# Five pairs of gate columns by a seven-product scheme in a two-block transformer kernel, with other buffer counts

## The chip, the cores and the metric

The kernel runs on one core of a Trainium2 chip, as one program in one launch. The metric is the device time of one execution in microseconds. Engines are named as in the profile: PE (TensorE), DVE (VectorE), ACT (ScalarE), POOL (GpSimd), SP (SyncE, which issues the weight loads).

## The reference, cut to what matters

Two transformer blocks over 512 tokens of width 1024 in fp32. The first block (a gated mixer with a delta rule, cross attention over a memory, a squared-ReLU feed-forward) is not touched by the change other than through buffer counts. The second block is:

```python
u = rmsnorm_2(x, norm_mix_w[l])
proj = u @ w_in[l] + b_in[l]
cb, cc, cx, q, k, v, g_conv, g_attn = jnp.split(proj, IN_SPLITS, axis=-1)
y_conv = (cb * causal_dwconv_2(cc * cx, conv_mix_w[l])) @ w_conv_out[l]
...
y_attn = sliding_window_attention(q, k, v, sinks[l]) @ w_attn_out[l] + b_attn_out[l]
merged = jax.nn.sigmoid(g_conv) * y_conv + jax.nn.sigmoid(g_attn) * y_attn
x = x + merged @ w_mix_out[l]
u = rmsnorm_2(x, norm_ffn_w[l])
up, gate = jnp.split(u @ w_ffn_up[l], 2, axis=-1)
a = causal_dwconv_2(up, ffn_conv_w[l], ffn_conv_b[l])
x = x + (jax.nn.silu(a) * gate) @ w_ffn_down[l]
```

The gates `g_conv` and `g_attn` are 1024 wide each: in columns of 128 they are columns 30 to 37 and 38 to 45 of `w_in_2`.

## The kernel before, in words

Activations are held transposed: a tile is 128 features by 512 tokens, and x is eight such tiles. Every matrix product runs in three matmuls per block of 128 x 128 weights (`mm3`, L480 to L484): weights and activations are split into a high part (rounded to fp32r) and a low part (the rest), and high x high, high x low and low x high are summed in PSUM. ACT makes the high part, DVE subtracts it to get the low part.

Weights come in units of eight blocks (128 x 1024), in one order written by `weight_order` (L60). SP loads them into NRAW = 4 raw buffers; `prefetch` (L256) splits them into one of NWS = 5 pairs of tiles `whi` and `wlo`. A plain column of `w_in_2` is one unit: eight blocks, 24 matmuls of 512 columns.

Two neighbouring columns can be a *pair*: `weight_order` lists it with `pair`, which orders the 16 blocks as quarters, and `pairg` (L367) computes it as a 2 x 2 block product with seven block products instead of eight (84 matmuls of 256 columns). For that, `seven_steps` (L309) forms two combinations of the weights (`sraw`, NSR = 2 buffers) and splits three tiles of 1024 and one of 512; `rights` (L413) forms the combinations of the activations, once for all pairs that share them, in steps s0 (two scalings by ACT), s1 (five short instructions of DVE) and s2 (two splits), for each two of the eight tiles. The seven products land in four PSUM banks (kind "mm" or "sm", four banks each), and L407 to L410 recombine them into a tile `q` of 1024 columns (NQ = 2 buffers), which a function `then` reads. Before the change pairs stand in the first block's feed-forward (14) and in the second one's (12, `SEVEN2`).

All tiles of 128 x 512 share one pool of NSLOT = 67 slots (`t2`, `tmp`, `acc_tile`). A slot is given when a tile is first written and comes free after its last reader.

What sets the order: the text issues instructions in its own order, `defer(n, f)` puts work n blocks of weights later, and the Tile framework then gives each engine a fixed order at build time, in which an instruction can run ahead of the text where its inputs are ready and it needs no new tile. SP alone keeps the order of the text. At run time each engine works through its queue in order.

In the second block's mixer, generators feed PE while the attention's chain waits (L1663 to L1667): `kvq_g`, `conv2_g` (columns 0 to 23), and `gated_g` (L1640): column 30, the eight columns of `w_conv_out_2`, then columns 31 to 37, each followed by a drain with rb (L1457), a sigmoid (L1659) and a product with `yc` (L1660). `norm_x` (L1441), eight instructions that apply the first block's last norm to x in place, is written beside them. Then (L1670 to L1677) each of columns 38 to 45 is followed by four blocks of `w_attn_out_2`, two DVE instructions with the gate (L1675, L1676) and a split of `yc` (L1677). The columns of `w_mix_out_2` follow (L1680), which add to x.

Of the kernel before, what the change touches and what calls it, by code (L numbers as in the profile page):

```python
# [13 lines left out]
AF = mybir.ActivationFunctionType  # L14
# [4 lines left out]
T = 512  # L19
D = 1024  # L20

NSLOT = 67
NRAW, NWS = 4, 5

NSR, NQ = 2, 2


SPREAD = [6, 2]
# [31 lines left out]
def weight_order():  # L60


    seq = []
    seven = set()

    def pair(name, n1, n2):
        assert len(seq) % 8 == 0
        seven.add(len(seq) // 8)
        for n, o in ((n1, 0), (n2, 1), (n1, 1), (n2, 0)):
            for k in range(o, 8, 2):  # L70
                seq.append((name, k, n))

    def cols(name, ns, ks):
        for n in ns:
            for k in ks:
                seq.append((name, k, n))

    def rows(name, ks, ns):
        for k in ks:
            for n in ns:  # L80
                seq.append((name, k, n))

    r8 = range(8)
    for lo in (12, 8, 16):
        cols("w_in", range(lo, lo + 4), r8)
    rows("w_in", r8, range(4, 8))
    cols("w_in", range(0, 4), r8)
    cols("w_in", range(20, 24), r8)
    cols("xa_wk", r8, r8)
    rows("xa_wv", r8, range(4))  # L90
    rows("xa_wv", r8, range(4, 8))
    cols("w_out", range(NWO), range(4))
    cols("w_out", range(NWO), range(4, 8))
    cols("w_out", range(NWO, 8), r8)
    cols("xa_wq", r8, r8)
    cols("xa_wo", range(4), range(6))
    cols("xa_wo", range(4), (6, 7))
    cols("xa_wo", range(4, 8), r8)
    for what, i, g in ffn_order():
        if what == 1 and i < NPLAIN:  # L100
            cols("ffn_w1", (2 * i, 2 * i + 1), r8)
        elif what == 1:
            pair("ffn_w1", 2 * i, 2 * i + 1)
        else:
            cols("ffn_w2", [i], range(8 * g, 8 * g + 8))

    cols("w_in_2", [28, 29, 24, 25, 26, 27], r8)
    for i in range(8):
        cols("w_in_2", [8 + i, 16 + i, i], r8)
    cols("w_in_2", [30], r8)  # L110
    cols("w_conv_out_2", r8, r8)
    cols("w_in_2", range(31, 38), r8)
    for i in range(8):
        cols("w_in_2", [38 + i], r8)
        cols("w_attn_out_2", [i], range(4))
    cols("w_mix_out_2", r8, r8)
    for what, i, g in ffn2_order():
        if what == 2:
            cols("w_ffn_down_2", [i], range(*GROUPS2[g]))
        elif i in SEVEN2:  # L120
            pair("w_ffn_up_2", i, 22 + i)
        else:
            cols("w_ffn_up_2", [i, 22 + i], r8)
    cols("w_ffn_down_2", r8, range(*GROUPS2[2]))
    return seq, seven
# [64 lines left out]
def _build(ctx, tc, nc, A, out, stage):  # L190
# [5 lines left out]
    V, S, G, PE = nc.vector, nc.scalar, nc.gpsimd, nc.tensor  # L196
    cnt = [0]

    def nm(s):
        cnt[0] += 1  # L200
        return f"{s}_{cnt[0]}"

    def t2(dt=F32, shape=(P, T)):
        return ap_.tile(list(shape), dt, tag="t2", bufs=NSLOT, name=nm("t2"))

    def ch(dt=F32):
        return ap_.tile([P, 4, P], dt, tag="t2", bufs=NSLOT, name=nm("ch"))

    def tmp(shape=(P, T)):
        return ap_.tile(list(shape), F32, tag="t2", bufs=NSLOT, name=nm("tmp"))  # L210

# [3 lines left out]
    def tinyc(n):  # L215
        return ap_.tile([P, n], F32, tag=nm("tinyc"), bufs=1, name=nm("tinyc"))
# [16 lines left out]
    def load_x():  # L233
        r = []
        for k in range(8):
            xt = ap_.tile([P, T], F32, tag="t2", bufs=NSLOT, name=nm("res"))
            nc.sync.dma_start(out=xt, in_=A["xT"][k])
# [3 lines left out]
    def col(name, i=0, n=1):  # L241
        o = COFF[name][0] + i
        return colt[:, o:o + n]
# [166 lines left out]
        V.tensor_tensor(q4[:, 1:3, :], b3(3), q4[:, 1:3, :], op=ALU.add)  # L410
        then(q)

    def rights(x, gname, xs):  # L413


        H = T // 2
        f = lambda hl, j: (hl[0][:, j * H:(j + 1) * H], hl[1][:, j * H:(j + 1) * H])
        res = [{} for _ in range(len(xs) // 2)]
        steps = []

        def one(p):
            st = {}

            def s0():
                st["a"], st["b"] = t2(), t2()
                S.activation(st["a"], x[2 * p], AF.Copy, scale=col(gname, 2 * p))
                S.activation(st["b"], x[2 * p + 1], AF.Copy, scale=col(gname, 2 * p + 1))

            def s1():
                a, b = st["a"], st["b"]  # L430
                st["v"], st["w"] = v, w = t2(), t2()
                V.tensor_sub(v[:, H:], b[:, H:], a[:, H:])
                V.scalar_tensor_tensor(out=w[:, :H], in0=a[:, H:], scalar=1.0, in1=a[:, :H],
                                       op0=ALU.mult, op1=ALU.subtract)
                V.tensor_scalar_mul(v[:, :H], w[:, :H], -1.0)
                V.tensor_sub(w[:, :H], w[:, :H], b[:, H:])
                V.scalar_tensor_tensor(out=w[:, H:], in0=w[:, :H], scalar=-1.0, in1=b[:, :H],
                                       op0=ALU.mult, op1=ALU.subtract)

            def s2():  # L440
                vs = split(st["v"])
                ws = split(st["w"])
                res[p].update({"B11": f(xs[2 * p], 0), "B21": f(xs[2 * p + 1], 0), "B22": f(xs[2 * p + 1], 1),
                               "V1": f(vs, 0), "V7": f(vs, 1), "V6": f(ws, 0), "T4": f(ws, 1)})

            return [s0, s1, s2]

        for p in range(len(xs) // 2):
            steps.extend(one(p))
        return res, steps  # L450
# [3 lines left out]
    def defer(n, fn):  # L454

        late.append((wst["i"] + n, fn))
        late.sort(key=lambda e: e[0])
# [99 lines left out]
    def zpad():  # L557
        zp = ap_.tile([P, T + 4], F32, tag="t2", bufs=NSLOT, name=nm("zp"))
        G.memset(zp[:, 0:4], 0.0)
        return zp  # L560
# [96 lines left out]
    xs = []  # L657
# [16 lines left out]
    rb = row_bc(rc, 4)  # L674
# [35 lines left out]
    for i in range(4):  # L710
        g = ap_.tile([P, T], F32, tag="t2", bufs=NSLOT, name=nm("gm"))
# [526 lines left out]
    xs = xs2  # L1238
# [86 lines left out]
    xs = xs2  # L1325
# [1 line left out]

    rb2 = acc_tile()
    wide_later(acc, 1e-6, rb2, WIDE1, True)
    rops, steps = rights(x, "norm_ffn", xs)  # L1330
    for j, f in enumerate(steps):
        defer(1 + VD * (j // 3) + j % 3, f)
    cosT, sinT = acc_tile(), acc_tile()
# [68 lines left out]
    gf2 = tinyc(8)  # L1402
    V.tensor_mul(gf2, col("norm_final", 0, 8), col("norm_mix_w_2", 0, 8))
    for what, n, g in ffn_order():
# [6 lines left out]
        t = tmp()  # L1411
# [11 lines left out]
    xs = xs2  # L1423

    rc12, rc, rb, rb1 = tinyc(8), tinyc(4), acc_tile(), acc_tile()
# [15 lines left out]
    def norm_x(n):  # L1441
        V.scalar_tensor_tensor(out=x[n], in0=x[n], scalar=col("norm_final", n), in1=rb1,
                               op0=ALU.mult, op1=ALU.mult)
# [8 lines left out]
    def proj_g(n):  # L1452

        ps = bank()
        yield from ling("w_in_2", n, range(8), xs, ps)
        t = tmp()
        V.tensor_mul(t, ps, rb)  # L1457
        return t

    def biased(n):  # L1460
        g = proj_g(n)
        while True:
            try:
                next(g)
            except StopIteration as e:
                return e.value

    def rope(n, t, then):

# [166 lines left out]
            cs_.append((hi, lo))  # L1636

    yc = []

    def gated_g():  # L1640
        sg0 = None
        for n in range(-1, 8):
            if n == -1:
                t = yield from proj_g(30)
                sg0 = t2()
                S.activation(sg0, t, AF.Sigmoid, bias=col("b_in_2", 30))
                continue
            ps = bank()
            yield from ling("w_conv_out_2", n, range(8), cs_, ps)
            y = t2()  # L1650
            if n == 0:
                V.tensor_mul(y, ps, sg0)
            else:
                S.copy(y, ps)
            yc.append(y)
        for i in range(1, 8):
            norm_x(i - 1)
            t = yield from proj_g(30 + i)
            S.activation(t, t, AF.Sigmoid, bias=col("b_in_2", 30 + i))  # L1659
            V.tensor_mul(yc[i], yc[i], t)  # L1660
        norm_x(7)

    bg.append(kvq_g())  # L1663
    bg.append(conv2_g())
# [3 lines left out]
    flush()  # L1668
    ms = []
    for i in range(8):  # L1670
        t = biased(38 + i)
        g = tmp()
        S.activation(g, t, AF.Sigmoid, bias=col("b_in_2", 38 + i))
        ps = lin("w_attn_out_2", i, range(4), at)
        V.scalar_tensor_tensor(out=g, in0=ps, scalar=col("b_attn_out_2", i), in1=g, op0=ALU.add, op1=ALU.mult)  # L1675
        V.tensor_add(yc[i], yc[i], g)  # L1676
        ms.append(split(yc[i]))  # L1677
# [9 lines left out]
    xs = xs2  # L1687


    rb = acc_tile()  # L1690
    wide_later(acc, 1e-5, rb, 8, False)

    rops2, steps = rights(x, "norm_ffn_w_2", xs)
    for j, f in enumerate(steps):
        defer(8 + 10 * (j // 3) + 2 * (j % 3), f)

# [39 lines left out]
    for what, n, g in ffn2_order():  # L1736
# [3 lines left out]
        a, b = GROUPS2[g]  # L1740
        ps = lin("w_ffn_down_2", n, range(a, b), hs)
        t = tmp()
# [7 lines left out]
    a, b = GROUPS2[2]  # L1750
# [27 lines left out]
    for hf in range(2):  # L1778
        ts = slice(hf * H, (hf + 1) * H)
# [3 lines left out]
        st = {}  # L1783
        for p in PAIRS:
            t = t2().rearrange("p (a b) -> p a b", a=2)
# [17 lines left out]
        for n in range(8):  # L1803
            part(n, range(nk - 1, nk) if hf == 0 and n < 3 else range(nk))
            xn = x[n][:, ts]
            t = tmp()
# [117 lines left out]
```

## Time and profile before

| what | us |
|---|---|
| median of 3 runs | 1541.34 |
| lowest, highest | 1540.96, 1542.74 |
| the profiled execution | 1543.6 |
| its span, first to last instruction | 1541.8 |

The profile is of one execution. Times of rows are microseconds from the span's start. PEld is PE's weight load, which runs beside its matmuls. A row of a timeline gives the start, the duration, the engine, the line, the operation, the tiles written and read, and in brackets how long the engine had idled before it and what ended that. Records of neighbouring instructions can overlap: the start of the next says how often one can begin.

### The profile page before, as it was taken

Reading aid. Unit: us, or ns where it says so; the run is one execution under the profiler, and the core shown is the slowest. Engines: PE = TensorE matmul, PEld = TensorE weight load, DVE = VectorE, ACT = ScalarE, POOL = GpSimd, SP = SyncE. Lnnn points to the kernel's source line nnn. Section 1 sums busy time; section 2 is a strip of 40 time slices with the busy share of each in tenths; the row PEclk is TensorE's granted clock in tenths of the full one; section 3 lists DMA queues with packets and bytes.
Section 4 is the critical chain, followed back from the end, with each engine's and each line's share of the span. In section 5 each row is a group of like instructions: output and inputs, shape, how many; then the busy total and the mean of one; then the engine's idle time right before and its main releaser. Section 6 shows DMA issues by size and latency. Waiting matters only on the chain.

```text
span 1541.8 us, 21393 instructions
## 1 busy us (share of the span) xinstructions
PE 1507.0 (98%) x8336; PEld 1290.3 (84%) x8336; DVE 1074.0 (70%) x1759; ACT 707.1 (46%) x1169; POOL 150.8 (10%) x162
## 2 busy tenths in 40 slices
PE   8999999999999999999999999999999998999996
PEld 6888898888888888989888888888888887898986
DVE  6897675554786786767688767335547887779757
ACT  5665555443564353535444434333334443344333
POOL 0002120200201202011400000000020001101201
PEclk9999999999999999999999999999999999999998
DMA  6033335221223223324044222222222222323311
GB/s 254 17 114 94 116 125 204 95 69 55 82 69 110 96 90 109 109 83 137 14 143 138 82 82 83 72 94 94 96 96 82 82 82 96 98 80 110 125 54 55
DMA packets 51509, 149.94 MB, mean 97 GB/s; under 512 B 9552, under 2 KB 14032, under 8 KB 51408
## 3 DMA queue, kind: packets, MB, share of 16 engines
q1 hardware_dynamic: 51264, 148.32, 28.5%
q8 instruction: 65, 1.06, 0.3%
q14 instruction: 36, 0.29, 0.1%
q10 hardware_dynamic: 144, 0.26, 0.1%
HBM read 143.97 MB, written 3.28 MB: 96 GB/s over the span
## 4 chain that ended last, share of the span: by engine, by line
PE 92%; DVE 4%; ACT 2%; issue 1%; DMA 1%; POOL 0%; SPq 0%; DVEq 0%; ACTq 0%; POOLq 0%
PE mm L482 26%; PE mm L483 25%; PE mm L484 25%; PE sm L484 3%; PE sm L482 3%; PE sm L483 3%; ACT whi L279 1%; DMA raw<-wts 1%; DVE wlo L281 0%; ACT t L1111 0%; PE sm L602 0%; DVE t L1825 0%; PE sm L920 0%; PE sm L1597 0%; PE sm L1596 0%
## 5 line engine op out<-in xcount | busy, mean ns | idle before, releaser
L482 PE MATMUL mm<-t,whi 128*128 128x512 f32 (+1 forms) x1840 | 686.0, 373 | 9.3 <-ACT whi L275 7.1
L483 PE MATMUL mm<-t,whi 128*128 128x512 f32 (+1 forms) x1840 | 682.9, 371 | 0.2 <-DVE t L551 0.2
L484 PE MATMUL mm<-t,wlo 128*128 128x512 f32 (+1 forms) x1840 | 682.5, 371 | 0.0
L482 PEld LDWEIGHTS mm<-t,whi 128*128 128x128 f32 x1840 | 347.4, 189 | 70.3 <-ACT whi L275 7.1
L484 PEld LDWEIGHTS mm<-t,wlo 128*128 128x128 f32 x1840 | 347.2, 189 | 63.3 <-DVE wlo L281 0.5
L483 PEld LDWEIGHTS mm<-t,whi 128*128 128x128 f32 x1840 | 347.4, 189 | 61.2 <-DVE t L551 0.7
L279 ACT CAST whi<-raw 128x1024 fp32r<-128x1024 f32 x202 | 211.2, 1051 | 303.6 <-PE mm L483 142.8
L281 DVE TENSOR_TENSOR wlo<-raw,whi 128x1024 fp32r<-128x1024 f32 x184 | 228.6, 1243 | 75.8 <-ACT whi L279 75.4
L596 POOL TENSOR_TENSOR acc<-acc,tmp 128x512 f32<-128x512 f32 (+1 forms) x37 | 52.7, 1430 | 467.7 <-ACT tmp L592 467.4
L482 PE MATMUL sm<-t,whi 128*128 128x256 f32 (+1 forms) x320 | 90.9, 284 | 2.9 <-ACT whi L326 2.9
L483 PE MATMUL sm<-t,whi 128*128 128x256 f32 (+1 forms) x320 | 90.8, 284 | 1.6 <-DVE t L551 1.6
L484 PE MATMUL sm<-t,wlo 128*128 128x256 f32 (+1 forms) x320 | 90.9, 284 | 0.8 <-DVE wlo L331 0.8
L331 DVE TENSOR_TENSOR wlo<-sraw,whi 128x1024 fp32r<-128x1024 f32 x52 | 68.8, 1325 | 30.9 <-ACT whi L326 30.6
L326 ACT CAST whi<-sraw 128x1024 fp32r<-128x1024 f32 x52 | 54.6, 1049 | 70.5 <-PE mm L483 59.9
L1457 DVE TENSOR_TENSOR tmp<-mm,acc 128x512 f32<-128x512 f32 x46 | 31.7, 690 | 49.0 <-PE mm L484 46.9
L482 PEld LDWEIGHTS sm<-t,whi 128*128 128x128 f32 x320 | 60.2, 188 | 4.0 <-ACT whi L326 3.3
L1414 POOL TENSOR_TENSOR res<-res,tmp 128x512 f32<-128x512 f32 x24 | 39.0, 1637 | 248.4 <-DVE tmp L1412 236.8
L483 PEld LDWEIGHTS sm<-t,whi 128*128 128x128 f32 x320 | 60.2, 188 | 2.5 <-DVE t L551 1.8
L484 PEld LDWEIGHTS sm<-t,wlo 128*128 128x128 f32 x320 | 60.4, 189 | 1.5 <-DVE wlo L331 1.0
L326 ACT CAST whi<-raw 128x1024 fp32r<-128x1024 f32 x26 | 27.3, 1050 | 51.7 <-PE mm L483 24.9
L318 DVE TENSOR_TENSOR sraw<-raw,raw 128x1024 f32<-128x1024 f32 x26 | 34.4, 1325 | 21.6 <-DMA raw<-wts 21.6
L1744 POOL TENSOR_TENSOR res<-res,tmp 128x512 f32<-128x512 f32 x16 | 27.6, 1734 | 164.9 <-DVE tmp L1743 164.9
(384 smaller groups left out, 1998.1 us busy)
## 6 DMA issues: line engine op xcount, KB each, us to landing
raw<-wts SPq DMA_DIRECT2D x259, 512.0 KB, 3.3
res<-xT SPq DMA_DIRECT2D x16, 256.0 KB, 5.2
yT<-t SPq DMA_DIRECT2D x6, 256.0 KB, 2.2
tmp<-tmp SPq DMA_DIRECT2D x20, 64.0 KB, 2.0
gm<-gm SPq DMA_DIRECT2D x4, 256.0 KB, 4.6
dn<-ch SPq DMA_DIRECT2D x4, 256.0 KB, 2.3
tmp<-memT SPq DMA_DIRECT2D x4, 256.0 KB, 2.6
cst<-const SPq DMA_DIRECT2D x1, 576.0 KB, 6.8
```

Source lines behind the costliest of these rows:

```text
L279: S.copy(hi, r)
L281: defer(LO, lambda r=r, hi=hi, lo=lo: V.tensor_sub(lo, r, hi.bitcast(F32)))
L318: V.tensor_tensor(t["s75"].rearrange("p (a b) -> p a b", a=2), r3, r1[:, T:].unsqueeze(1).to_broadcast([P, 2, T]), op=ALU.add)
L326: S.copy(t[n][0], s)
L331: V.tensor_sub(t[n][1], src(), t[n][0].bitcast(F32))
L482: PE.matmul(ps, lhsT=ahi, rhs=bhi, start=start, stop=False)
L483: PE.matmul(ps, lhsT=ahi, rhs=blo, start=False, stop=False)
L484: PE.matmul(ps, lhsT=alo, rhs=bhi, start=False, stop=stop)
L596: eng.tensor_add(acc[:, :w], acc[:, :w], dst[:, :w])
L1414: G.tensor_add(x[n], x[n], t)
L1457: V.tensor_mul(t, ps, rb)
L1744: G.tensor_add(x[n], x[n], t)
```

## The change

Columns 34/35 and 36/37 of the convolution's gate and 38/39, 40/41 and 42/43 of the attention's gate become pairs; columns 31, 32, 33, 44 and 45 stay plain. For the attention's gate the order becomes one pair, then the eight blocks of `w_attn_out_2` of both columns. `rights` is called for the second block's x with the combined scale `gf2`, its steps deferred from column 31 on, and all eight `norm_x` are written after the two pairs of `gated_g`. NWS goes from 5 to 6, NQ from 2 to 1, NSLOT from 67 to 65.

```diff
-NSLOT = 67
-NRAW, NWS = 4, 5
-
-NSR, NQ = 2, 2
+NSLOT = 65
+NRAW, NWS = 4, 6
+
+NSR, NQ = 2, 1
...
-    cols("w_in_2", range(31, 38), r8)
-    for i in range(8):
+    cols("w_in_2", (31, 32, 33), r8)
+    for i in (34, 36):
+        pair("w_in_2", i, i + 1)
+    for i in range(0, 8, 2):
+        if i < 6:
+            pair("w_in_2", 38 + i, 39 + i)
+            cols("w_attn_out_2", [i, i + 1], range(4))
+    for i in (6, 7):
         cols("w_in_2", [38 + i], r8)
         cols("w_attn_out_2", [i], range(4))
...
-    def rights(x, gname, xs):
+    def rights(x, gcol, xs):
...
-                S.activation(st["a"], x[2 * p], AF.Copy, scale=col(gname, 2 * p))
-                S.activation(st["b"], x[2 * p + 1], AF.Copy, scale=col(gname, 2 * p + 1))
+                S.activation(st["a"], x[2 * p], AF.Copy, scale=gcol(2 * p))
+                S.activation(st["b"], x[2 * p + 1], AF.Copy, scale=gcol(2 * p + 1))
...
-    def biased(n):
-        g = proj_g(n)
+    def run(g):
         while True:
             try:
                 next(g)
             except StopIteration as e:
                 return e.value
+
+    def biased(n):
+        return run(proj_g(n))
...
+    ropsg = []
+
+    def proj2_g(n, kind):
+
+        r = []
+
+        def then(q):
+            for j in range(2):
+                t = tmp()
+                V.tensor_mul(t, q[:, j * T:(j + 1) * T], rb)
+                S.activation(t, t, AF.Sigmoid, bias=col("b_in_2", n + j), scale=1.0 - 2 * j)
+                r.append(t)
+
+        yield from pairg("w_in_2", n, n + 1, ropsg, then, kind)
+        return r
...
-        for i in range(1, 8):
-            norm_x(i - 1)
+        res, steps = rights(x, lambda n: gf2[:, n:n + 1], xs)
+        ropsg.extend(res)
+        for j, f in enumerate(steps):
+            defer(1 + 5 * (j // 3) + j % 3, f)
+        for i in (1, 2, 3):
             t = yield from proj_g(30 + i)
             S.activation(t, t, AF.Sigmoid, bias=col("b_in_2", 30 + i))
             V.tensor_mul(yc[i], yc[i], t)
-        norm_x(7)
+        for i in (4, 6):
+            ts = yield from proj2_g(30 + i, "mm" if i == 4 else "sm")
+            for j in range(2):
+                V.tensor_mul(yc[i + j], yc[i + j], ts[j])
+        for i in range(8):
+            norm_x(i)
...
-        t = biased(38 + i)
-        g = tmp()
-        S.activation(g, t, AF.Sigmoid, bias=col("b_in_2", 38 + i))
+        if i < 6:
+            if i % 2 == 0:
+                gates = list(run(proj2_g(38 + i, "sm" if i % 4 else "mm")))
+            g = gates[i % 2]
+        else:
+            t = biased(38 + i)
+            g = tmp()
+            S.activation(g, t, AF.Sigmoid, bias=col("b_in_2", 38 + i))
```

## Rows read from the trace of the kernel before

**Rows 1.** The page's first part: busy time, share and instructions of each engine.

```profile
PE 1507.0 (98%) x8336; PEld 1290.3 (84%) x8336; DVE 1074.0 (70%) x1759; ACT 707.1 (46%) x1169; POOL 150.8 (10%) x162
```

**Rows 2.** Stretches (length, then busy PE, PEld, DVE, ACT, POOL; PEclk; DMA share; GB/s).

```profile
1009.80:1026.50 16.70, 16.70 (x74) 13.54 (x73) 6.63 (x8) 6.23 (x8) 0.00 (x0) 1.00 0.28 95
1026.50:1054.00 27.50, 27.50 (x120) 22.32 (x119) 12.33 (x15) 8.08 (x11) 0.00 (x0) 1.00 0.27 96
1054.00:1120.00 66.00, 66.00 (x286) 53.35 (x286) 36.61 (x44) 22.81 (x28) 0.00 (x0) 1.00 0.28 92
```

**Rows 3.** Timeline of ACT: the sigmoids after two neighbouring plain columns.

```profile
1032.56 0.72 ACT L1659 ACTIVATE tmp<-tmp,colt 128x512 f32<-128x512 f32 x1
...
1038.12 0.71 ACT L1659 ACTIVATE tmp<-tmp,colt 128x512 f32<-128x512 f32 x1
```

**Rows 4.** Timeline of PE: the first matmuls of three pairs in a row.

```profile
524.76 0.28 PE L482 MATMUL mm<-t,whi 128*128 128x256 f32 x1
...
534.70 0.28 PE L482 MATMUL sm<-t,whi 128*128 128x256 f32 x1
...
544.62 0.28 PE L482 MATMUL mm<-t,whi 128*128 128x256 f32 x1
```

**Rows 5.** Stretches, columns as in rows 2: three pairs in a row, at two places.

```profile
435.45:470.65 35.20, 31.60 (x257) 30.70 (x256) 31.34 (x40) 23.91 (x35) 0.00 (x0) 1.00 0.34 116
524.76:555.34 30.58, 29.94 (x254) 29.73 (x252) 22.96 (x27) 17.53 (x25) 1.30 (x1) 1.00 0.34 113
```

**Rows 6.** Timeline of DVE, back to back, with the start of a recombination.

```profile
545.61 0.69 DVE L331 TENSOR_TENSOR t<-raw,t 128x512 fp32r<-128x512 f32 x1
546.21 0.68 DVE L407 TENSOR_TENSOR q<-sm,t 128x512 f32<-128x512 f32 x1
546.81 1.22 DVE L281 TENSOR_TENSOR wlo<-raw,whi 128x1024 fp32r<-128x1024 f32 x1
547.94 0.68 DVE L408 TENSOR_TENSOR q<-sm,q 128x512 f32<-128x512 f32 x1
548.66 0.42 DVE L409 TENSOR_TENSOR q<-sm,q 128x256 f32<-128x256 f32 x1
549.12 0.69 DVE L410 TENSOR_TENSOR q<-sm,q 128x512 f32<-128x512 f32 x1
```

**Rows 7.** Timeline of DVE: first and last of the five instructions of s1.

```profile
434.29 0.42 DVE L432 TENSOR_TENSOR t<-t,t 128x256 f32<-128x256 f32 x1
...
435.87 0.42 DVE L437 SCALAR_TENSOR_TENSOR t<-t,t 128x256 f32<-128x256 f32 x1
```

**Rows 8.** Timeline of DVE: seven of the eight `norm_x`.

```profile
770.05 4.73 DVE L1442 SCALAR_TENSOR_TENSOR res<-res,colt,acc 128x512 f32<-128x512 f32 x7 [0.21 <-ACT acc L612]
```

**Rows 9.** Timeline of ACT: a split and the second s0 before the last feed-forward.

```profile
1186.17 0.62 ACT L550 CAST t<-tmp 128x512 fp32r<-128x512 f32 x1 [0.76 <-DVE tmp L1732]
1186.70 0.72 ACT L426 ACTIVATE t<-res,colt 128x512 f32<-128x512 f32 x1
```

**Rows 10.** Timeline of PE: matmuls after idle gaps, in both feed-forwards.

```profile
470.31 0.38 PE L482 MATMUL sm<-t,whi 128*128 128x256 f32 x1 [1.84 <-ACT whi L326]
...
555.34 0.50 PE L482 MATMUL mm<-t,whi 128*128 128x512 f32 x1 [0.64 <-ACT t L401]
...
1276.26 0.39 PE L482 MATMUL sm<-t,whi 128*128 128x256 f32 x1 [1.02 <-ACT whi L326]
...
1277.60 0.38 PE L484 MATMUL sm<-t,wlo 128*128 128x256 f32 x1 [0.83 <-DVE wlo L331]
...
1283.08 0.55 PE L482 MATMUL mm<-t,t 128*128 128x256 f32 x1 [4.03 <-DVE tmp L1743]
```

**Rows 11.** Timeline of ACT: a split after idle time, in the last feed-forward.

```profile
1275.16 1.04 ACT L326 CAST whi<-raw 128x1024 fp32r<-128x1024 f32 x1 [3.28 <-PE mm L483]
```

**Rows 12.** A stretch, columns as in rows 2, after the last gap of rows 10.

```profile
1283.08:1289.30 6.22, 6.22 (x29) 6.19 (x30) 1.05 (x2) 0.00 (x0) 2.86 (x3) 0.50 0.25 87
```

**Rows 13.** Timeline of DVE: the readers of one q and the next pair's first write.

```profile
554.25 1.29 DVE L1384 TENSOR_TENSOR t<-q,t 128x512 fp32r<-128x512 f32 x2
555.45 0.68 DVE L407 TENSOR_TENSOR q<-mm,t 128x512 f32<-128x512 f32 x1
```

More of the change, by code (lines that the diff above doesn't have):

```diff
@@ L1329, in _build @@
     wide_later(acc, 1e-6, rb2, WIDE1, True)
-    rops, steps = rights(x, "norm_ffn", xs)
+    rops, steps = rights(x, lambda n: col("norm_ffn", n), xs)
     for j, f in enumerate(steps):
@@ L1691, in _build @@
     wide_later(acc, 1e-5, rb, 8, False)
-    rops2, steps = rights(x, "norm_ffn_w_2", xs)
+    rops2, steps = rights(x, lambda n: col("norm_ffn_w_2", n), xs)
     for j, f in enumerate(steps):
```

## The prediction, made before the change was run

> **What bounds the kernel now.** I read the busy shares first: TensorE is busy 1507.0 of 1541.8 us, VectorE 70% [rows 1]. So only two things can shorten the run: fewer TensorE microseconds, or fewer of the 35 us in which it stands. Then I asked for the stages around the change. From the last `w_conv_out_2` column (1009.8) to the end of the `w_attn_out_2` loop (1120), TensorE is busy in every microsecond, while VectorE is busy 6.63 + 12.33 + 36.61 = 55.6 of 110.2 us and ScalarE 37.1 [rows 2]. The reader is to see a stage bound by TensorE alone, with half of VectorE free. The timelines then give prices, and the idle gaps of TensorE show where pairs of columns by seven products already cost more than their matmuls.
>
> **The change, part by part.**
>
> *The products.* A plain column of 24 matmuls of 512 columns takes 1038.12 - 1032.56 = 5.56 us, read from the sigmoids that follow two neighbouring columns [rows 3]; two columns 11.12 us. A pair by seven products is 84 matmuls of 256 columns. Pairs in a row start at 524.76, 534.70 and 544.62 [rows 4]: 9.93 us each. So a pair returns 1.19 us, and five pairs (34/35, 36/37, 38/39, 40/41, 42/43) **-5.95 us** of TensorE's own work. The weights are the same blocks in another order: the bytes moved do not change.
>
> [...]
>
> *VectorE's work.* Back to back, instructions of 512 elements start 0.60 us apart and those of 1024 elements 1.13 us (545.61, 546.21, 546.81, 547.94), although their records last 0.69 and 1.22 us [rows 6]. Preparing a pair is four instructions of 1024 (the sum s75, three low parts) and three of 512 (s6, s4, the low part of b): 4 x 1.13 + 3 x 0.60 = 6.32 us. Recombining is three of 512 and one of 256, 3 x 0.60 + 0.33 = 2.13 us (0.33 taken as half a 512 plus its share of overhead; the row has 0.46 with its dependency). Two products with rb add 1.2 us. That is 9.65 us per pair, where two plain columns take two low parts and two drains, 3.46 us: +6.2, and 31 us for five. The new `rights` needs, per pair of rows of x, five short instructions in 435.87 + 0.42 - 434.29 = 2.0 us [rows 7] and two low parts of 512, so 4 x 3.2 = 12.8 us.
>
> The eight `norm_x` move. They are written beside columns 31 to 37 but ran at 770.05, 4.73 us for seven [rows 8]: the framework hands each engine what is ready, not what is next in the text. Now they must stay behind `rights`, which reads x as it was before them, so 5.4 us move into the busy stage. The steps of `rights` cannot be drawn forward as far: they take slots of the shared pool, and slots are given in the order of the text. The same steps before block 2's feed-forward show it: the second pair's first instruction (L426) starts right behind the split (L550) written ahead of it, at 1186.70 after 1186.17 [rows 9]. So `rights` starts when the last convolution column has its slot, about 1010.
>
> From there to the start of the last pair, TensorE has 3 x 5.56 + 3 x 9.93 + 5.56 + 9.93 + 5.56 = 67.5 us of matmuls as cover. VectorE has: `rights` 12.8; low parts of columns 32 and 33, 2.3; drains and products of 31 to 33, 3.6; preparation of five pairs, 31.6; recombination and rb of three pairs, 10.0; their products with yc, 2.4; four attention columns at three instructions, 7.2; two low parts of attention weights, 2.3. Sum 72.2 us: TensorE waits some **+4.6 us** for VectorE in all. With the eight `norm_x` ahead of the last pair it would be 10. From below: three pairs in a row, prepared without `rights`, lost 30.58 - 3 x 9.93 = 0.8 us; three in a row right after `rights` lost 35.20 - 29.79 = 5.4 us [rows 5]. The second row is the nearest, as `rights` falls together with three pairs in both; 4.6 lies beside it. Bounds 0.8 and 10.
>
> *ScalarE.* A pair adds about 2 us of splits, `rights` 10 us in all: 37 + 20 of 110 us. Nothing waits for that as long as VectorE is the later of the two; if it were not, it would be the same wait under another name. The queue of the weight loads is moved past nothing.
>
> *Sixth pair of split buffers (NWS).* A pair needs three wide splits, so two pairs fit in six. [...] With a buffer free the split starts earlier; I take the two first gaps and the loss at the low clock, 1.85 + 2.79 = **-4.6 us**, and leave the 4.03, whose order has nothing to do with buffers. Best case: all of it, and the 1.84 at 470.31, -10.5. Worst: the new order makes one more such place, +8.7.
>
> *Two slots fewer (NSLOT), one q (NQ).* The hidden activations of both feed-forwards nearly fill the pool by my count of the code. The one gap whose waited-for instruction takes a slot of its own is the 0.64 us at 555.34, behind the copy c0 [rows 10]. One such gap, **+0.7 us**; bounds 0 and, were it at each of five group ends, 3.2. For q, the last instructions that read it (L1384 at 554.25) stand in VectorE's queue right ahead of the next pair's first write (L407 at 555.45) [rows 13]: one buffer keeps that order at no cost. If that cover is gone, the recombination waits 1.2 us, and the other four PSUM banks let TensorE go on.
>
> **Sum.** -5.95 + 4.6 - 4.6 + 0.7 = -5.25 us. The profiled execution took 1543.6 us, 1.8 around its span and 2.3 above the median of the runs; it would become 1538.3, and the median 1541.3 becomes **1536.1 us**.
>
> **Rivals.**
> 1. *The stage gives back what the products save.* VectorE loses 5.4 us as in the row after `rights`, and the sixth buffer moves no gap, since the largest one is an order in VectorE's queue. -5.95 + 5.4 + 0.7: 1541.5. For it: VectorE would need 105 of 110 us. Chance 0.25.
> 2. *VectorE becomes the bound (slower).* If its instructions follow each other at the length of their records (0.69 and 1.22 us [rows 6]) because most wait for ScalarE or for the one before, the 72.2 us become 72.2 x 1.13 = 82, and TensorE waits 14 us before the last pair. -5.95 + 14 - 4.6 + 0.7: about 1545.6, and 1550 without the buffer's gain. It decides once VectorE is later than some 9 us at pair 42. Against it: while behind, VectorE started at 0.60 and 1.13 us. Chance 0.16. [...]
> 3. *The stalls go too.* Pairs lose only 0.8 us, the buffer frees all 10.5: -5.95 + 0.8 - 10.5: 1525.7. Chance 0.13.
> 4. *Seven products cost more than they save,* because each weight load needs its own time: 13.54 us for 73 loads [rows 2] is 185 ns, 84 loads 15.6 us, +4.5 per pair, 1564. In pairs 252 loads fit in 29.73 us [rows 5]. Chance 0.01; the first rule above would end on this side.
>
> **How the numbers follow.** The forecast has 0.45, with a range of its own from 1532 to 1540. What a measurement can tell from no change is about 0.2%, 3 us. Faster: nearly all of the forecast and rival 3, 0.58. Same: rival 1 less a little, and the upper edge of the forecast, 0.24. Slower: rivals 2 and 4 and the upper end of rival 1, 0.18. The range of 1528 to 1545.5 leaves out most of rival 3, the worse half of rival 2 and rival 4.
>
> **What would show it.** Right: pairs 34 and 36 at about 9.93 us once started; a gap of a few us ahead of the second product of pair 34; VectorE near full from 1010 to 1075; `norm_x` after 1010; no stretch at half clock near 1276. Wrong: no gap at pair 34 (then VectorE's count is too high), or a gap over 4 us there with a fallen clock, new gaps in block 1's feed-forward (slots), or the gaps of [rows 10] unchanged.

## The result, and the profile after

The changed kernel takes 1551.57 us (median of 4 runs) against 1542.04 before (4 runs): a ratio of 1.0058, 95% interval 1.0045 to 1.0071. It is slower by 9.5 us, where 5 us less were forecast.

In the rows below and in the experiments two lines serve as milestones: the last drain of the first block's feed-forward, and the first sum with `w_mix_out_2`. Between them lie the projections, the attention and the gates of the second block. The answers for single lines give the first and last start of their instructions; first the kernel before, then the changed one.

```profile
L1412 DVE TENSOR_TENSOR tmp<-mm,acc x32: 678/688/693, 480.6 to 759.3; 128x512 f32<-128x512 f32 x32
L1682 DVE TENSOR_TENSOR res<-res,mm x8: 686/689/690, 1120.9 to 1159.8; 128x512 f32<-128x512 f32 x8
L1743 DVE TENSOR_TENSOR tmp<-mm,acc x16: 678/684/693, 1282.2 to 1470.9; 128x512 f32<-128x512 f32 x16
```

```profile
L1418 DVE TENSOR_TENSOR tmp<-mm,acc x32: 678/684/693, 482.6 to 760.1; 128x512 f32<-128x512 f32 x32
L1718 DVE TENSOR_TENSOR res<-res,mm x8: 686/689/689, 1131.0 to 1170.0; 128x512 f32<-128x512 f32 x8
L1779 DVE TENSOR_TENSOR tmp<-mm,acc x16: 678/684/693, 1288.7 to 1478.6; 128x512 f32<-128x512 f32 x16
```

The first milestone moved by 0.8 us. The *gate stage* between the milestones grew from 1120.9 - 759.3 = 361.6 to 370.9 us: +9.3. From there to the first drain of the second feed-forward (L1743 before, L1779 after) the time fell from 161.3 to 157.7 us: -3.6. From that drain to the end of the span it grew from 259.6 to 261.1 us: +1.5, with new gaps of 0.93 and 1.28 us (at 1311 and 1329) and, behind gaps of 0.30, 0.49 and 0.82 us at 1417 to 1420, a granted clock of 0.50 until 1423.8. The four parts make the 8.0 us by which the spans of the two profiled executions differ; the medians differ by 9.5.

Five pairs should have made the gate stage 5.95 us shorter, so some 15 us were lost in it. PE's timeline shows where; these are the only gaps over 0.3 us there.

```profile
1035.82 0.58 PE L488 MATMUL mm<-t,t 128*128 128x256 f32 x1 [3.09 <-DVE res L1448]
...
1037.09 0.58 PE L490 MATMUL mm<-t,t 128*128 128x256 f32 x1 [0.47 <-DVE t L337]
...
1095.25 0.58 PE L488 MATMUL mm<-t,t 128*128 128x256 f32 x1 [6.04 <-ACT t L332]
```

The columns of the stretches are those of [rows 2].

```profile
1032.57:1035.82 3.25, 0.16 (x2) 0.00 (x0) 3.25 (x7) 2.65 (x5) 0.00 (x0) 0.82 0.00 0
1035.82:1041.50 5.68, 5.21 (x22) 4.88 (x23) 5.48 (x13) 2.03 (x4) 0.00 (x0) 0.50 0.29 92
1041.50:1084.80 43.30, 43.30 (x323) 41.22 (x323) 37.47 (x52) 21.16 (x28) 0.00 (x0) 1.00 0.30 98
...
1089.05:1095.25 6.20, 0.16 (x2) 0.00 (x0) 6.04 (x9) 4.02 (x7) 0.00 (x0) 0.79 0.65 233
1095.25:1099.50 4.25, 4.25 (x19) 4.10 (x20) 0.81 (x2) 0.22 (x1) 0.00 (x0) 0.50 0.33 123
```

The reader is to see two gaps, each followed by a stretch at a granted clock of 0.50, and 43 full microseconds between them, with the rest of pair 34, three whole pairs and two units of `w_attn_out_2`. Behind the second gap 19 matmuls take 4.25 us instead of 19 x 0.118 = 2.2 (9.93 / 84 = 0.118 us each in the pairs of [rows 4]), so the low clock costs 2.0 us; behind the first, some 24 matmuls (22 have a record) take 5.21 us instead of 24 x 0.118 = 2.8, which costs 2.4. Together 3.09 + 0.47 + 2.4 + 6.04 + 2.0 = 14.0 us. -5.95 + 14.0 = 8.1 of the 9.3; the remaining 1.2 us are within what the first milestone differs by between traces whose first block is the same and has the same counts (759.3 before, 757.7 in e2 and 760.3 in e12 below).

Both gaps end with a matmul `mm<-t,t`. Only one of the seven products has its weights in tiles of the shared pool: that with b, the one piece of 512 that is split into `t2` tiles (now L332 on ACT for the high part, L337 on DVE for the low part). So both gaps wait for the split of b. At the first gap the wait is put down to a `norm_x` (L1448), whose record happens to end at that moment and which writes nothing that this matmul reads; the high part of b, which it does read, is ready 0.05 us before it starts (1035.17 + 0.60). What stands ahead of b on ACT, at the first gap and at the second, and then on DVE at the second:

```profile
1034.54 0.72 ACT L1685 ACTIVATE tmp<-tmp,colt 128x512 f32<-128x512 f32 x1 [0.56 <-DVE tmp L1463]
1035.17 0.60 ACT L332 CAST t<-raw 128x512 fp32r<-128x512 f32 x1
...
1090.12 1.33 ACT L1657 ACTIVATE tmp<-tmp,colt 128x512 f32<-128x512 f32 x2
1093.51 1.17 ACT L556 CAST t<-t 128x512 fp32r<-128x512 f32 x2 [2.06 <-DVE t L1712]
1094.59 0.61 ACT L332 CAST t<-raw 128x512 fp32r<-128x512 f32 x1
```

```profile
1071.49 0.69 DVE L345 TENSOR_TENSOR sraw<-sraw,raw 128x512 f32<-128x512 f32 x1
...
1083.42 0.69 DVE L413 TENSOR_TENSOR q<-sm,t 128x512 f32<-128x512 f32 x1 [4.64 <-PE sm L490]
...
1089.08 1.29 DVE L1656 TENSOR_TENSOR tmp<-q,acc 128x512 f32<-128x512 f32 x2
...
1091.42 1.40 DVE L1711 SCALAR_TENSOR_TENSOR tmp<-mm,colt,tmp 128x512 f32<-128x512 f32 x2
1092.74 1.28 DVE L1712 TENSOR_TENSOR t<-t,tmp 128x512 f32<-128x512 f32 x2
...
1095.38 0.68 DVE L337 TENSOR_TENSOR t<-raw,t 128x512 fp32r<-128x512 f32 x1
1101.91 0.69 DVE L413 TENSOR_TENSOR q<-mm,t 128x512 f32<-128x512 f32 x1 [5.85 <-PE mm L490]
```

The chain runs from the recombination of pair 40 (L413, 1083.42) over the products with rb (L1656), the sigmoids (L1657), the gate (L1711, L1712) and the splits of `yc` (L556) to the split of b for pair 42 (L332). The weights of that pair have nothing to do with `yc`, and they were not late: the last of the pair's sums (L345), which reads the same half of the raw buffer as b's split, ran at 1071.49, 23 us earlier. But b's slot is given behind theirs, because in the text the last steps of a pair's preparation come after the loop has handled the two attention columns. And DVE is not short of time: it idles 4.64 us before this chain and 5.85 us behind it. At the first gap DVE is busy throughout. One `norm_x` (L1448) stands ahead of the drain of column 32 (L1463), on which the sigmoid ahead of b's high part waits, and two more ahead of b's low part (L337):

```profile
1032.56 0.74 DVE L1448 SCALAR_TENSOR_TENSOR res<-res,colt,acc 128x512 f32<-128x512 f32 x1
1033.22 0.69 DVE L557 TENSOR_TENSOR t<-t,t 128x512 fp32r<-128x512 f32 x1
1033.82 0.68 DVE L1463 TENSOR_TENSOR tmp<-mm,acc 128x512 f32<-128x512 f32 x1
1034.42 1.41 DVE L1448 SCALAR_TENSOR_TENSOR res<-res,colt,acc 128x512 f32<-128x512 f32 x2
1035.74 0.68 DVE L1686 TENSOR_TENSOR t<-t,tmp 128x512 f32<-128x512 f32 x1
1036.35 0.68 DVE L337 TENSOR_TENSOR t<-raw,t 128x512 fp32r<-128x512 f32 x1
```

### The profile page after: what moved, and what is told of

Its sections match the earlier page's. It is cut to its first block, busy times and chain, and to the rows that moved or that the text cites. A ratio compares the mean times of both kernels' runs of the same rounds, so it can differ in the third digit from the quotient of the medians.

```text
span 1549.8 us, 21917 instructions
## 1 busy us (share of the span) xinstructions
PE 1507.9 (97%) x8516; PEld 1298.1 (84%) x8516; DVE 1109.1 (72%) x1832; ACT 726.0 (47%) x1200; POOL 152.3 (10%) x162
## 4 chain that ended last, share of the span: by engine, by line
PE 89%; DVE 7%; ACT 2%; issue 1%; DMA 1%; POOL 0%; SPq 0%; DVEq 0%; ACTq 0%
PE mm L488 24%; PE mm L490 24%; PE mm L489 24%; PE sm L490 4%; PE sm L489 4%; PE sm L488 4%; DVE wlo L287 1%; DVE wlo L337 1%; DMA raw<-wts 1%; ACT whi L285 0%; ACT t L1117 0%; DVE t L337 0%; DVE t L1861 0%; DVE tmp L1616 0%; ACT whi L332 0%
## 5 line engine op out<-in xcount | busy, mean ns | idle before, releaser
L488 PE MATMUL mm<-t,whi 128*128 128x512 f32 (+1 forms) x1832 | 675.4, 369 | 8.3 <-ACT whi L281 7.5
L489 PE MATMUL mm<-t,whi 128*128 128x512 f32 (+1 forms) x1832 | 671.9, 367 | 0.5 <-DVE t L557 0.5
L490 PE MATMUL mm<-t,wlo 128*128 128x512 f32 (+1 forms) x1832 | 671.6, 367 | 0.1
L287 DVE TENSOR_TENSOR wlo<-raw,whi 128x1024 fp32r<-128x1024 f32 x171 | 212.3, 1242 | 51.5 <-ACT whi L285 51.0
L332 ACT CAST whi<-sraw 128x1024 fp32r<-128x1024 f32 x62 | 65.1, 1050 | 101.9 <-PE mm L489 82.3
L490 PE MATMUL sm<-t,wlo 128*128 128x256 f32 (+1 forms) x368 | 104.6, 284 | 2.1 <-DVE wlo L337 2.1
L337 DVE TENSOR_TENSOR wlo<-sraw,whi 128x1024 fp32r<-128x1024 f32 x62 | 80.7, 1302 | 34.2 <-ACT whi L332 34.2
L489 PE MATMUL sm<-t,whi 128*128 128x256 f32 (+1 forms) x368 | 104.4, 284 | 0.7 <-DVE t L557 0.7
L488 PE MATMUL sm<-t,whi 128*128 128x256 f32 (+1 forms) x368 | 104.4, 284 | 0.3 <-ACT whi L332 0.3
L489 PEld LDWEIGHTS sm<-t,whi 128*128 128x128 f32 x368 | 69.3, 188 | 1.6 <-DVE t L557 0.9
L488 PEld LDWEIGHTS sm<-t,whi 128*128 128x128 f32 x368 | 69.3, 188 | 1.2 <-ACT whi L332 0.5
L1420 POOL TENSOR_TENSOR res<-res,tmp 128x512 f32<-128x512 f32 x24 | 40.2, 1693 | 248.9 <-DVE tmp L1418 239.5
L332 ACT CAST whi<-raw 128x1024 fp32r<-128x1024 f32 x31 | 32.6, 1052 | 51.5 <-PE mm L489 31.8
L488 PE MATMUL mm<-t,t 128*128 128x256 f32 x144 | 42.7, 297 | 11.9 <-ACT t L332 8.7
L324 DVE TENSOR_TENSOR sraw<-raw,raw 128x1024 f32<-128x1024 f32 x31 | 39.3, 1267 | 11.9 <-DMA raw<-wts 11.7
L337 DVE TENSOR_TENSOR wlo<-raw,whi 128x1024 fp32r<-128x1024 f32 x31 | 38.9, 1255 | 12.2 <-ACT whi L332 12.2
```

The lines of the kernel that those rows point to most:

```text
L287: defer(LO, lambda r=r, hi=hi, lo=lo: V.tensor_sub(lo, r, hi.bitcast(F32)))
L324: V.tensor_tensor(t["s75"].rearrange("p (a b) -> p a b", a=2), r3, r1[:, T:].unsqueeze(1).to_broadcast([P, 2, T]), op=ALU.add)
L332: S.copy(t[n][0], s)
L337: V.tensor_sub(t[n][1], src(), t[n][0].bitcast(F32))
L488: PE.matmul(ps, lhsT=ahi, rhs=bhi, start=start, stop=False)
L489: PE.matmul(ps, lhsT=ahi, rhs=blo, start=False, stop=False)
```

## The experiments

Theory A, *order*: the split of b stands late in its queues. Theory B, *amount*: VectorE has too much to do in the gate stage. Theory C, *buffers*: the three counts cost the time. Times are medians; each ratio is to the kernel before, run on the same chip in the same rounds (1542.3 to 1542.6 us).

**e1_buffers**: the kernel before, with the counts alone.

```diff
-NSLOT = 67
-NRAW, NWS = 4, 5
-NSR, NQ = 2, 2
+NSLOT = 65
+NRAW, NWS = 4, 6
+NSR, NQ = 2, 1
```

> The kernel before with the three buffer counts of the change alone (NWS 6, NQ 1, NSLOT 65), no pair of gates. Theory A (order: in the gate stage the split of b stands late in its queues, because its slot is given in the order of the text, and TensorE's clock falls behind the gap) and theory B (amount: VectorE has too much work in the gate stage) both expect little: the stages outside the gates differ by -0.9, +1.7, +0.8 and -2.3 us in the changed kernel's trace, in all about -0.7, so 1541 us. Theory C (the buffer counts cost the time): 1546 us or more.

Measured 1543.24 us, ratio 1.0002 (0.9993 to 1.0010): no difference. Theory C falls. The parts show why it is not simply nothing:

```profile
L1682 DVE TENSOR_TENSOR res<-res,mm x8: 686/689/689, 1122.6 to 1161.5; 128x512 f32<-128x512 f32 x8
L1743 DVE TENSOR_TENSOR tmp<-mm,acc x16: 678/684/693, 1280.2 to 1469.0; 128x512 f32<-128x512 f32 x16
```

1280.2 - 1122.6 = 157.6 us, as in the changed kernel and 3.7 less than before: of the gaps of [rows 10] at 1276 to 1283 one of 0.67 us is left. Behind that drain the half clock of [rows 12] is gone too (1.00 as a mean from 1270 to 1300), but new gaps of 0.78 and 1.24 us come in at 1302 and 1321, and from the drain to the end of the span both kernels need the same (259.6 and 259.9 us). In the first block it is the other way round: the gap at 441.84, 1.54 us before, is 2.69 us (at 442.64), with a granted clock of 0.50 from 444.4 to 447.8, and the block ends 1.3 us later (760.6). The span of the profiled execution is 1.7 us shorter, but the medians show no such difference: this execution took 1542.28, 1.0 us less than e1's median, and that of the kernel before 1543.6, more than 1 us above its own.

**e2_oldbuf**: the changed kernel with NWS 5, NQ 2 and NSLOT 67.

> The changed kernel with the buffer counts of before (NWS 5, NQ 2, NSLOT 67). Theories A and B: the gate stage keeps its two gaps (3.6 and 6.0 us) and its half clock, 1549 to 1554 us. Theory C: near 1536 us, the saving of the products without the loss.

Measured 1551.50 us, ratio 1.0062 (1.0047 to 1.0076). The gate stage takes 1126.9 - 757.7 = 369.2 us, with gaps of 2.71 and 4.05 us, and three smaller ones of 0.43 to 0.76 us, at the same two pairs. The loss belongs to the pairs, not to the counts.

**e3_bfirst**: the split of b is written with the first two steps of a gate pair's preparation.

```diff
+        if order[u * 8][0] == "w_in_2":
+            return op, [
+                both(s75, hi("a", a), hi("b", b)),
+                both(lo("a", a), hi("s75s", c), lo("b", b)),
+                both(s6, s4),
+                both(lo("s75s", c), hi("s64s", d)),
+                both(lo("s64s", d), end),
+            ]
```

> The changed kernel, but in the gates' five pairs the split of b (the fourth weight block row, 512 wide) is written with the first steps of the preparation instead of the last. Same instructions, another order. Theory A: the gap of 6.0 us ahead of pair 42 goes, with the 2 us that the half clock behind it costs, and the one at pair 34 (3.6 us) shrinks to 2 us or less: 1540 to 1544 us. Theory B: VectorE has the same work, so the gaps move to other products and the total stays at 1549 to 1552 us.

Measured 1541.84 us, ratio 0.9996 (0.9988 to 1.0005). The same instructions in another order are 9.7 us faster than the changed kernel (0.9996 against 1.0058 of the kernel before). On ACT, b of pair 42 is now split ahead of the sigmoids (L1665) and of the splits of `yc` (L564):

```profile
1084.57 0.61 ACT L332 CAST t<-raw 128x512 fp32r<-128x512 f32 x1
1085.09 1.34 ACT L1665 ACTIVATE tmp<-tmp,colt 128x512 f32<-128x512 f32 x2
...
1088.94 1.13 ACT L564 CAST t<-t 128x512 fp32r<-128x512 f32 x2
```

The gap at pair 42 is gone, and at pair 34 these are left (and one of 0.28 us), with part of the stretch behind them at the low clock:

```profile
1033.09 0.39 PE L497 MATMUL mm<-t,whi 128*128 128x256 f32 x1 [0.33 <-DVE t L565]
...
1035.96 0.42 PE L496 MATMUL mm<-t,t 128*128 128x256 f32 x1 [2.13 <-DVE tmp L1471]
```

```profile
1036.00:1041.50 5.50, 5.50 (x34) 5.50 (x35) 4.76 (x11) 2.43 (x4) 0.00 (x0) 0.69 0.00 0
```

Theory A holds for pair 42: the place of b in the text decides. That it does so through the slot is read from the kernel, as the sums of the same preparation, which take no slot of that pool, did run ahead (L345 above); no run varies the slot alone. What is left at pair 34 is no longer the split of b, which ran at 1024.18 on ACT, but a drain:

```profile
1035.22 0.69 DVE L1471 TENSOR_TENSOR tmp<-mm,acc 128x512 f32<-128x512 f32 x1
```

It is the second of the three in this stage, so that of column 32, and comes some 13 us after that column's last matmul. The product with b is the third of its pair to take a PSUM bank; by the kernel's text, with four banks "mm" in turn, that is the bank of column 32, and its first matmul starts 0.05 us after the drain ends. The gate stage still takes 361.5 us, 5.8 more than 361.6 - 5.95.

**e4_normpool**: `norm_x` taken off VectorE.

```diff
-        V.scalar_tensor_tensor(out=x[n], in0=x[n], scalar=col("norm_final", n), in1=rb1,
-                               op0=ALU.mult, op1=ALU.mult)
+        S.activation(x[n], x[n], AF.Copy, scale=col("norm_final", n))
+        G.tensor_mul(x[n], x[n], rb1)
```

> The changed kernel with the eight norm_x taken off VectorE: ScalarE scales, GpSimd multiplies. It takes 5.4 us of VectorE out of the gate stage. Theory A: the gap at pair 34 shrinks from 3.6 to about 1 us (three norm_x stand ahead of the low part of b there), the gap of 6.0 us at pair 42 stays: 1546 to 1549 us. Theory B: both shrink by what VectorE saves, and no half clock is left: 1541 to 1544 us.

Measured 1554.80 us, ratio 1.0074 (1.0062 to 1.0086): slower than both theories said. The gap at pair 42 stays (6.01 us), against theory B. At pair 34 there are now three, of 2.24, 0.89 and 1.81 us, two of them behind splits of `rights` on ACT (L556), ahead of which ACT's queue has the new scalings (L1448):

```profile
1027.75 1.33 ACT L1448 ACTIVATE res<-res,colt 128x512 f32<-128x512 f32 x2
1028.98 1.04 ACT L332 CAST whi<-sraw 128x1024 fp32r<-128x1024 f32 x1
1031.44 0.62 ACT L556 CAST t<-t 128x512 fp32r<-128x512 f32 x1 [1.41 <-DVE t L441]
...
1037.99 1.33 ACT L1448 ACTIVATE res<-res,colt 128x512 f32<-128x512 f32 x2
1042.14 0.62 ACT L556 CAST t<-t 128x512 fp32r<-128x512 f32 x1 [2.81 <-DVE t L441]
```

As a test of amount it is confounded, since it loads ACT in the same place. e9 asks the question again without that.

**e9_late_only**: the changed kernel with `norm_x` held back, by letting it read a copy of its row factor that is made after pair 42.

```diff
-        for i in range(8):
-            norm_x(i)
...
+        if i == 6:
+            S.copy(rb1b, rb1)
+            for n in range(8):
+                norm_x(n)
```

> The changed kernel with norm_x held back as in e6_normlate, and the split of b where the change has it. Takes 5.4 us of VectorE out of the stretch ahead of pair 42 without giving ScalarE more. Theory A (order): the gap of 6.0 us at pair 42 stays, as the split of b still stands behind the splits of yc; only the loss at pair 34 shrinks: 1545 to 1549 us. Theory B (amount): both gaps shrink or go, 1538 to 1543 us.

Measured 1547.73 us, ratio 1.0033 (1.0020 to 1.0045), in theory A's interval. With 5.4 us of VectorE gone from the stretch, pair 34 waits 0.91 and 0.32 us, with a granted clock of 1.00 from 1034 to 1040; pair 42 waits as before:

```profile
1033.94 0.39 PE L488 MATMUL mm<-t,t 128*128 128x256 f32 x1 [0.91 <-ACT t L332]
...
1034.75 0.39 PE L490 MATMUL mm<-t,t 128*128 128x256 f32 x1 [0.32 <-DVE t L337]
...
1091.17 0.58 PE L488 MATMUL mm<-t,t 128*128 128x256 f32 x1 [6.07 <-ACT t L332]
```

```profile
1091.17:1095.50 4.33, 4.33 (x19) 4.24 (x20) 0.75 (x2) 0.21 (x1) 0.00 (x0) 0.50 0.37 121
```

So the two gaps have two causes: at pair 42 order alone, at pair 34 order together with the lead that VectorE has there.

**e6_normlate**: e3_bfirst with `norm_x` held back as in e9.

> e3_bfirst with the eight norm_x held back: they read a copy of their row factor that is made only after pair 42, so that they run beside columns 44 and 45. From the last convolution drain to the first sum with w_mix_out, e3_bfirst took 109.8 us, where matmuls alone need 104.7. Theory A2 (what is left is VectorE's queue ahead of pair 34, into which norm_x was put): the gap of 2.1 us at pair 34 and its half clock go, 105 to 107 us, total 1536 to 1539 us. Theory B2 (the work of rights itself is too late, norm_x only fills holes): 109 us, total unchanged at 1541 to 1543 us.

Measured 1538.20 us, ratio 0.9967 (0.9954 to 0.9979). The gap at pair 34 is 1.11 us, with a granted clock of 1.00 behind it; it ends with the drain of column 32, which now starts at 1034.16. The gate stage takes 358.2 us.

**e7_early**: e3_bfirst with `rights` written one column earlier.

```diff
+            if n == 7:
+                res, steps = rights(x, lambda n: gf2[:, n:n + 1], xs)
+                ropsg.extend(res)
+                for j, f in enumerate(steps):
+                    defer(1 + 5 * (j // 3) + j % 3, f)
             ps = bank()
             yield from ling("w_conv_out_2", n, range(8), cs_, ps)
```

> e3_bfirst with rights written one column earlier, beside the last column of w_conv_out_2 instead of column 31, so that VectorE begins 5.6 us sooner; norm_x as in the change. Theory B2: the gap at pair 34 goes, 105 to 107 us for the stage, total 1536 to 1539 us. Theory A2: norm_x still stands in the queue, but 5.6 us more lead cover it too: 106 to 108 us. If the slots of the pool do not allow the earlier start, nothing moves: 110 us and 1542 us.

Measured 1538.21 us, ratio 0.9965 (0.9951 to 0.9978); the gate stage takes 357.0 us, and no gap is left at pair 34. The first scaling of `rights` starts at 1007.9 instead of 1012.3, and all eight `norm_x` still run ahead of the pair's product with b (1008.7 to 1029.4 on VectorE). The drain of column 32 does not come earlier than in e3:

```profile
1036.58 1.28 DVE L1471 TENSOR_TENSOR tmp<-mm,acc 128x512 f32<-128x512 f32 x2
```

The product with b starts behind the first of these two, at 1037.32. But until then TensorE has other work: 30 matmuls of other products of pairs 34 and 36 start between 1033.6 and 1037.2, where e3 stood still. So e6 brings the drain forward, and e7 gives TensorE something to do while it waits for it, most likely because `rights` delivers the combinations of x sooner; which of them e3 lacked stays open. A2 and B2 are both right in part.

**e8_lateearly**: e3_bfirst with both edits.

> e3_bfirst with both: rights one column earlier and norm_x beside columns 44 and 45. Theories A2 and B2 both expect the stage at its matmuls, 105 us, and 1536 to 1538 us in all; if it stays above 107 us, a third cause holds TensorE back there.

Measured 1536.57 us, ratio 0.9955 (0.9942 to 0.9969): faster than both kernels, 15.0 us less than the change. TensorE has no idle time left from pair 34 to the first sum with `w_mix_out_2`, while VectorE is busy 96.8 of 106.6 us by its records:

```profile
L1426 DVE TENSOR_TENSOR tmp<-mm,acc x32: 676/684/693, 482.8 to 760.3; 128x512 f32<-128x512 f32 x32
L1729 DVE TENSOR_TENSOR res<-res,mm x8: 686/687/689, 1116.6 to 1155.7; 128x512 f32<-128x512 f32 x8
```

```profile
1010.00:1060.00 50.00, 50.00 (x340) 46.09 (x339) 45.47 (x71) 30.26 (x42) 0.00 (x0) 1.00 0.24 75
1060.00:1116.60 56.60, 56.60 (x328) 49.67 (x328) 51.28 (x71) 24.55 (x34) 0.00 (x0) 1.00 0.39 130
```

The gate stage takes 356.3 us, 5.3 less than before: the five pairs do return about what their matmuls save. Compared with e1, which has the same counts (1122.6 - 760.6 = 362.0 us), it is 5.7.

**e12_oldbuf**: e8_lateearly with NWS 5, NQ 2 and NSLOT 67.

> e8_lateearly with the buffer counts of before (NWS 5, NQ 2, NSLOT 67). If the gates' pairs do not need the sixth split buffer, the time from the first block's end to the first sum with w_mix_out stays at 356 to 358 us (356.3 in e8_lateearly), block 1 ends some 2 us earlier and the second feed-forward loses the 3.7 us that it gained: 1537 to 1539 us. If they need it, new gaps appear between 1025 and 1100 and the total is over 1541 us.

Measured 1537.84 us, ratio 0.9966 (0.9953 to 0.9978). The gate stage takes 1116.1 - 760.3 = 355.8 us: the gates' pairs do not need the sixth split buffer. The second feed-forward again has its gaps of 1.02, 1.27 and 4.03 us. The first block did not end earlier (760.3), so that part of what was expected fell.

**e11_before_ball**: the kernel before, with b first in the pairs of both feed-forwards.

> The kernel before with the split of b written first in the 26 pairs of the two feed-forwards; no pair of gates. In before, products with b wait 1.54 us at 441.84 and 4.03 us at 1283.08, the second with 2.8 us lost at half clock behind it. Theory A (the place of b in the text decides): both gaps shrink, 1534 to 1538 us. Rival: the feed-forwards' pairs wait for other things as well (buffers, the last low part), and an earlier b only moves the gap: 1540 to 1543 us.

Measured 1539.66 us, ratio 0.9981 (0.9972 to 0.9990), between the two forecasts. The gap at 441.84 is gone, but that at 470.31 grew from 1.84 to 2.36 us, and the clock falls behind it: matmuls of 512 columns start 0.43 us apart up to 472.0 and 0.23 us apart from there on. The gap of 4.03 us shrinks to 1.12, and what is left ends with a drain (L1751); 1.06 and 1.53 us ahead of it remain, which wait for splits of the three wide pieces, and the clock still falls behind them: 0.89 as a mean from 1265 to 1295. The place of b is a real term there too, worth about half of what was expected. No run has the same edit on top of e8_lateearly.

## Why the prediction was wrong

*The products* were right: -5.95 forecast, -5.3 to -5.7 measured once nothing waits (e8). Rival 4 falls with that, and no run shows a rule that would end on its side.

*VectorE's work* is the step that failed. It was priced at +4.6 us with an upper bound of 10; TensorE's waits and the low clock behind them measured 14.0. The count of 72 us of work against 67.5 us of cover treated VectorE as a sum: work is late only if there is too much of it. The count was even too high, as the three sums of pair 34 (L324, L342, L345), which it places in the stage, ran at 981 to 986, and still the wait was longer. The runs show that the place in the queue decided. At pair 42 VectorE idled on both sides of a gap of 6.0 us, and e3 removed that gap without removing an instruction. At pair 34 it was the split of b and, behind it, the late drain of column 32. The prediction had read from [rows 9] that slots are given in the order of the text, and used it only to say when `rights` can begin. It did not ask the same of the other tiles that the new pairs take from the pool; among the operands of the seven products b's are the only ones. That the drain is late for the same reason, its `tmp` being a slot of the pool too, is likely and was not tested.

The prediction had a wait of this kind before it. It took the last gap of [rows 10], 4.03 us before a matmul `mm<-t,t`, for an order in VectorE's queue that has nothing to do with buffers. But L482 reads high parts only, which ACT makes. The row names a drain (L1743), and b's high part had come 0.8 us ahead of it:

```profile
1281.51 0.61 ACT L326 CAST t<-raw 128x512 fp32r<-128x512 f32 x1
...
1282.24 0.68 DVE L1743 TENSOR_TENSOR tmp<-mm,acc 128x512 f32<-128x512 f32 x1
```

With b first the gap is 1.12 us (e11), with the three counts alone it is gone (e1).

Two smaller parts of that step: the sum left `norm_x` out of what stands ahead of the last pair. It ran from 1013 to 1038, seven of the eight ahead of the low part of b for pair 34 (e9 against the change: 3.8 us). And the fall of the clock behind each new gap was not priced, although [rows 12] had its price: 4.4 of the 14.0 us.

*The buffers* were mis-sized, by less: the sixth buffer at -4.6, slots and q at +0.7, -3.9 in all. The -4.6 is the gaps of 1.02 and 0.83 us of [rows 10] and, from [rows 12], the loss at the clock of 0.50, 6.22 - 29 x 0.118 = 2.79. No run shows it by itself: the three counts were not varied one by one, so what can be compared is their sum. From the first sum with `w_mix_out_2` to the end of the span the changed kernel gained 2.1 us (-3.6 and +1.5, above) and e1 3.4. The half clock near 1283 is gone (1.00 as a mean from 1283 to 1300 in the changed kernel). But of the two gaps that were to go one went and the other is still 0.68 us, and the 4.03 us that were left in the sum went too. Elsewhere the new order costs time, as the prediction had it in its worst case: in the first block (442.64 in e1) and late in the second feed-forward. Over the whole kernel e1 shows no difference, 1.0002, and e8 is 1.3 us below e12, the same kernel with the old counts, which their intervals do not separate.

*Rivals.* Rival 2 (VectorE the bound, 1545.6 to 1550) had the right side and nearly the time, for a reason that the runs refute: in e7, with `norm_x` in place, TensorE has no gap over 0.25 us in the whole gate stage, so VectorE's work fits when it starts in time and in the right order. The records of 0.69 and 0.68 us at 1033.22 and 1033.82 above, 0.60 us from start to start, show again that the length of a record is not how often an instruction begins. Rival 1 had the right idea, that the stage gives back what the products save, and too small a loss.

## What to carry to other kernels

Where a framework orders the queues, look for what ties a new piece of work to the text: here a slot of a shared pool, which put the split of a weight behind a chain of activations that it does not need. Before counting an engine's microseconds, list for each new operand what must be issued before it and how long that chain is; a queue can be half empty and still late. When a gap is found, check which operand the waiting matmul reads, and which PSUM bank it writes: here an operand named by its pool led to the first cause, and the drain of an earlier column that used the bank to the second.

## What the runs showed of the hardware that was not expected

A gap cost more than its length. Behind gaps of 6.04 and 3.09 us the granted clock was 0.50, and 4.4 us went there on top; behind 2.13 us (e3) the mean over the next 5.5 us was 0.69, behind 1.11 us (e6) it stayed at 1.00. So to shorten a gap from 2.1 to 1.1 us brought more than the difference: the gate stage fell by 3.3 us from e3 to e6, in which two gaps of 0.28 and 0.33 us went as well. The length of a gap alone does not say whether the clock falls: behind the gap of 1.84 us of [rows 10] it stayed at 1.00, behind one of 1.85 us at the same place in e12 it fell. The stretches, the kernel before and then e12:

```profile
470.31:474.00 3.69, 3.69 (x17) 3.05 (x18) 3.69 (x6) 0.22 (x1) 0.00 (x0) 1.00 0.36 107
...
469.81:473.35 3.54, 3.54 (x10) 2.86 (x11) 3.54 (x5) 0.21 (x1) 0.00 (x0) 0.52 0.32 93
```
